# A hybrid convolution and attention block on one core: spectrum, values and output gates laid out in DRAM by the order of their loads

## The chip, the cores and the metric

The kernel runs on one core of a Trainium2 chip. The metric is the device time of one execution in microseconds (us), the median over several runs. The engines are TensorE (PE, matrix products), VectorE (DVE), ScalarE (ACT), GpSimd (POOL) and SyncE (SP). SP issues nearly all transfers between DRAM and the on-chip memory; ACT issues a few. Sixteen DMA engines carry them out, in packets of one contiguous run each.

## The reference

One block works on 2048 tokens of width 1024, with 256 context tokens and a conditioning vector. Half of the width goes through a gated long convolution, the other half through gated linear attention (4 heads, keys of 64, values of 128, both directions). Then come an output projection and an MLP of 4096.

```
spec = _hyena_spectrum(T, ...)        # rfft of a generated filter of 512 channels
u, q, k, v, og, gk = split(h @ w_in)  # widths 1536, 256, 256, 512, 512, 16+16
y1 = x0 * (irfft(rfft(x1 * v1) * spec) + bias)
y2 = gla_bidir(q, k, v, log_gate(gk)) normalized * silu(og)
x  = x + gate * ([y1, y2] @ w_out)
x  = x + gate * (relu(norm(x) @ w1)**2 @ w2)
```

## The kernel before, in words

Matrix products that need full precision are made of three products of rounded halves (`mm3`, lines 226 to 228). The stages, in time: the spectrum of the filter with the context beside it (0 to 232 us), the projections (226 to 821), the convolution with the attention woven in (821 to 1126), the output projection (to 1400), the MLP (to the end). Each stage is written as Python generators that take turns by weights; a scheduler then orders each engine's instructions within that, and pools of buffers with a fixed count set how far a load can run ahead.

**Spectrum.** `kernel_steps` goes twice over 256 of the 512 channels (`hc`). In 16 steps each it makes two blocks of 128 frequency rows, `ks` (line 640), 128 partitions by 2 x 256 numbers, and stores them to the DRAM tensor `d_s` (line 649). Rows 0 to 63 of a block are real parts, rows 64 to 127 imaginary parts. `d_s` is `[32, 128, 512]`: block, row, channel. The first step (`t == 0`) stores its blocks apart: row 127 of block 0 goes to `d_s0` and is filled with zeros in `d_s` (lines 644, 645), rows 0 to 126 of block 0 by line 646, and block 1 by line 647.

**Values, gates.** The columns of the input projection for values (512), output gates (512) and decay gates (32) are held as four groups of 264, `wi_vg`. `token_major` multiplies each group with 16 blocks of 128 tokens; a value goes to `d_v`, an output gate through Silu (ACT, line 694) and a product with the norm's weights (POOL, line 695) to `d_og`, both `[2048, 512]`, token by column. Since 264 does not divide 512, group 1 holds 248 columns of values and 16 of gates, and group 3 holds the 32 decay columns, copied to `gs` (line 698).

**Convolution.** For each half of the channels: a forward transform (`ua1`, `ua2`), a loop of 16 steps over the frequency blocks, an inverse transform. A step of the loop is staged over `k0` (loads), `k1`, `k2`, `k3`. `k0` loads the transforms' coefficients `dff` and `dfi` at every second step (lines 917, 919), and the step's spectrum to two tiles, `kr` and `ki`, of 128 partitions by 512 numbers (lines 923, 924). Both halves of a tile's partitions hold the same 64 rows, so there are four loads a step, each of 64 partitions by 2 runs of 256 numbers. `k2` makes the forward product on PE (`pu`, line 945), then `kr*pu` on DVE (line 951), `sw*ki` on POOL (line 952) and their sum on DVE (line 953); `k3` is the inverse product on PE (`p`, line 962). There are 5 buffers for `kr`, 3 for `ki`, 2 for `dff`, 3 for `dfi`.

**Attention.** In turns with that, for each of 4 heads: `kt` and `vv` (keys, values) are loaded once (1 MB each, lines 826 and 830), `qi`, `ki<-d_ki` and `dc` (lines 1055 to 1058), and for each quarter of the tokens the gates `og` (256 KB, line 1112). The loads of `vv` and `og` read 128 numbers of a token at a time.

All these loads stand in one queue on SP, in program order. A load that waits, for its buffer for one, holds all that stand behind it. Besides, each transfer takes one of eight semaphores in turn and waits until the transfer eight places ahead of it has landed.

Of the kernel before, what the change touches and what calls it, by code (L numbers as in the profile page):

```python
# [124 lines left out]
def layout(x):  # L125

    f4 = np.float32
    c = constants()
    x = {k: np.asarray(v) for k, v in x.items()}
    o = {"x": x["x"][0], "ctx": x["ctx"][0], "norm_final": x["norm_final"], "gla_norm": x["gla_norm"][0],  # L130
         "w_out": x["w_out"][0]}
    col = lambda v: v.reshape(-1, P).T
    prm = np.zeros((P, NPRM), f4)
    for at, v in ((SILC, x["c"]), (SILC + 8, x["c_ctx"]), (B_ADA, x["b_ada"]), (NMIX, x["norm_mix"]),
                  (NMLP, x["norm_mlp"]), (CONVW, x["conv_w"]), (CONVB, x["conv_b"]), (HB, x["hyena_bias"]),
                  (GKB, x["gk_b_fwd"]), (GKB + 2, x["gk_b_bwd"])):
        v = col(v)
        prm[:, at:at + v.shape[1]] = v
    for i, nm in enumerate(("filt_b1", "filt_b2", "filt_b3", "filt_freq")):
        prm[:64, FLT + i] = prm[64:, FLT + i] = x[nm][0]  # L140
    prm[:, TKC:TKC + 32] = c["tk"]
    prm[:, IDC:IDC + P] = c["ident"]
    o["prm"] = prm
    fpk = np.zeros((P, 1536), f4)
    for i, nm in enumerate(("filt_w1", "filt_w2", "filt_w3")):
        w = x[nm][0]
        n = w.shape[0]
        fpk[0:n, i * P:i * P + 64] = w
        fpk[n:2 * n, i * P + 64:(i + 1) * P] = w
    fpk[:64, 384:896] = x["filt_wout"][0][:, :DH]  # L150
    fpk[64:, 384:896] = x["filt_wout"][0][:, DH:]
    fpk[:, 896:1024] = c["dft_k"]
    fpk[:, 1024:1536] = c["negdelta"]
    o["fpk"] = fpk
    gw = np.zeros((P, 2, 256), f4)
    for i in range(4):
        gw[32 * i:32 * i + 16, 0] = x["gk_w_fwd"][0]
        gw[32 * i + 16:32 * i + 32, 1] = x["gk_w_bwd"][0]
    o["gw"] = gw
    blk = lambda w: np.ascontiguousarray(w.reshape(-1, P, w.shape[1]).transpose(1, 0, 2))  # L160
    wa = x["w_ada"][0]
    o["wada1"] = np.stack([blk(wa[:, i * 256:(i + 1) * 256]) for i in range(8)])
    o["wada2"] = np.stack([blk(wa[:, 2 * D + i * P:2 * D + (i + 1) * P]) for i in range(32)])
    wi = x["w_in"][0]
    o["wi_vg"] = np.stack([blk(wi[:, 2048 + i * 264:2048 + (i + 1) * 264]) for i in range(4)])
    two = lambda a, b: np.concatenate([blk(wi[:, a:a + P]), blk(wi[:, b:b + P])], axis=2)
    o["wi_qk"] = np.stack([two(1536 + i * P, 1792 + i * P) for i in range(2)])
    o["wi_xv"] = np.stack([two(512 + i * P, 1024 + i * P) for i in range(4)])
    o["wi_x0"] = np.stack([blk(wi[:, i * P:(i + 1) * P]) for i in range(4)])

    w1 = x["w_mlp1"][0].reshape(2, 4, P, 16, 2, P)
    o["w1"] = np.stack([np.stack([w1[l, :, :, n, i].transpose(1, 0, 2).reshape(P, 512)
                                  for i, l in ((0, 0), (0, 1), (1, 1), (1, 0))], axis=1) for n in range(16)])

    w2 = x["w_mlp2"][0].reshape(16, 2, P, 2, 512)
    o["w2"] = np.stack([np.stack([w2[n, i, :, j] for i, j in ((0, 0), (1, 0), (1, 1), (0, 1))], axis=1)
                        for n in range(16)])
    for n in ("zt", "dft_u", "dft_f", "dft_i", "dft_y", "reset", "attm"):
        o[n] = c[n]
    return {k: np.ascontiguousarray(v) for k, v in o.items()}  # L180
# [30 lines left out]
def hybrid_block(ctx: ExitStack, tc, a, out, dbg=None):  # L211
# [20 lines left out]
        dve.tensor_sub(lo, src, hi.bitcast(F32))  # L232

    dr = ctx.enter_context(tc.tile_pool(name="dram", bufs=1, space=DRAM))
    d_s = dr.tile([32, 128, DH], F32, name="d_s")
    d_s0 = dr.tile([1, DH], F32, name="d_s0")
    d_q = dr.tile([2, 256, T], F32, name="d_q")
    d_ki = dr.tile([2, 256, T], F32, name="d_ki")
    d_kt = dr.tile([NH, P, 16, 2, 64], F32, name="d_kt")
    d_dec = dr.tile([2, 256, 32], F32, name="d_dec")  # L240
    d_v = dr.tile([T, 512], F32, name="d_v")
    d_og = dr.tile([T, 512], F32, name="d_og")
    d_u = dr.tile([DH, T], F32, name="d_u")
    d_x0 = dr.tile([DH, T], F32, name="d_x0")
    d_yt = dr.tile([D, T], F32, name="d_yt")
# [108 lines left out]
    with ExitStack() as ek:  # L354
# [114 lines left out]
        def context_steps():  # L469
# [11 lines left out]
            yield from norm_out(xc, hch, hcl, 1)  # L481
            vc = xp.tile([P, 2, 512], F32, name="vc")
            gc = xp.tile([P, 2, 32], F32, name="gc")
            for g_, c0, n in ((3, 232, 32), (0, 0, 264), (1, 0, 264)):
                hi, lo = load_w(a["wi_vg"][g_][:, :, c0:c0 + n])
                for i in range(2):
                    pp = pt("pc")
                    for k in range(KD):
                        ts = slice(i * P, (i + 1) * P)
                        mm3(pp[:, 0:n], hch[:, k, ts], hcl[:, k, ts], hi[:, k, 0:n], lo[:, k, 0:n],  # L490
                            k == 0, k == KD - 1)
                    if g_ == 0:
                        nc.scalar.copy(vc[:, i, 0:264], pp[:, 0:264])
                    elif g_ == 1:
                        nc.scalar.copy(vc[:, i, 264:512], pp[:, 0:248])
                    else:
                        nc.scalar.copy(gc[:, i, :], pp[:, 0:32])
                    yield W["c_proj"]
# [57 lines left out]
        def kernel_steps():  # L556
            for hc in range(2):
# [73 lines left out]
                def second(t):  # L631
# [10 lines left out]
                    if t == 0:  # L642

                        dma(d_s0[:, cs], k3[127:128, 0, :])
                        dma(d_s[0, 127:128, cs], zrow[0:1, :])
                        dma(d_s[0, 0:127, cs], k3[0:127, 0, :])
                        dma(d_s[1, :, cs], k3[:, 1, :])
                    else:
                        dma(d_s[kk:kk + 2, :, cs].rearrange("k p c -> p k c"), k3)

                yield from staged(16, fetch, turn, second, w=W["k_turn"])

# [16 lines left out]
    rst = ap.tile([P, 512], F32, name="rst")  # L669
    dma(rst[:], a["reset"])  # L670

    def token_major(grp, w, tbs):

        c0 = 264 * grp
        hi, lo = w
        vn = max(0, min(264, 512 - c0))
        on = min(1024 - c0, 264) - vn
        o0 = max(0, c0 - 512)
        for tb in tbs:
            if grp == 3:  # L680
                gs = ap.tile([P, 4, 32], F32, tag="gs", bufs=2, name="gs")
            for i in range(4):
                pp = pt("pv")
                ts = slice(i * P, (i + 1) * P)
                for k in range(KD):
                    mm3(pp[:, 0:264], hts[tb][0][:, k, ts], hts[tb][1][:, k, ts], hi[:, k, :], lo[:, k, :],
                        k == 0, k == KD - 1)
                rows = slice(tb * 512 + i * P, tb * 512 + (i + 1) * P)
                st = ap.tile([P, 512], F32, tag=("gt1", "glg")[i % 2], bufs=2, name="st")
                if vn:  # L690
                    dve.tensor_copy(st[:, 0:vn], pp[:, 0:vn])
                    dma(d_v[rows, c0:c0 + vn], st[:, 0:vn])
                if on:
                    act(st[:, vn:vn + on], pp[:, vn:vn + on], AF.Silu)
                    gps.tensor_mul(st[:, vn:vn + on], st[:, vn:vn + on], gnf[:, o0:o0 + on])
                    dma(d_og[rows, o0:o0 + on], st[:, vn:vn + on])
                if grp == 3:
                    dve.tensor_copy(gs[:, i, :], pp[:, 232:264])
                yield 2.7
            if grp == 3:  # L700
                pg = pt("pg")
                for i in range(4):
                    tr(pg[0:32, i * P:(i + 1) * P], gs[:, i, :], ident)
                dve.tensor_copy(gt[tb * 32:(tb + 1) * 32, :], pg[0:32, :])

    def mod_block(j):
# [116 lines left out]
    def load_kv(h, part=None):  # L823
        if part != 1:
            kt = pre.tile([P, 16, 2, 64], F32, tag="kt", bufs=1, name="kt")
            dma(kt[:], d_kt[h])
            heads[h, "kt"] = kt
        if part != 0:
            vv = gpool(h).tile([P, 16, P], F32, tag="vv", bufs=1, name="vv")
            dma(vv[:], d_v[:, h * P:(h + 1) * P].rearrange("(b p) e -> p b e", p=P))  # L830
            heads[h, "kv"] = (heads[h, "kt"], vv)

    def load_u(ct):
# [48 lines left out]
    def conv_steps():  # L882
        for hc in range(2):
# [29 lines left out]
            def k0(t):  # L913
# [4 lines left out]
                    st["i", t // 2] = ft("dfi", 3, "dfi")  # L918
                    dma(st["i", t // 2][:], a["dft_i"][:, kk:kk + 4, :].rearrange("p k n -> p (k n)"))
                kr, ki = ft("kr", 5, "kr"), ft("ki", 3, "ki")  # L920
                for h in range(2):
                    hs = slice(h * 64, (h + 1) * 64)
                    dma(kr[hs].rearrange("p (k c) -> p k c", k=2), d_s[kk:kk + 2, 0:64, cs].rearrange("k p c -> p k c"))
                    dma(ki[hs].rearrange("p (k c) -> p k c", k=2), d_s[kk:kk + 2, 64:128, cs].rearrange("k p c -> p k c"))
                if t == 0:
                    dma(kr[127:128, 0:256], d_s0[:, cs])
                st["k", t] = (kr, ki)
# [181 lines left out]

    def load_og(h, q):  # L1110
        og = gp.tile([P, 4, P], F32, tag="og", bufs=4, name="og")
        dma(og[:], d_og[q * DH:(q + 1) * DH, h * P:(h + 1) * P].rearrange("(b p) e -> p b e", p=P))
        heads[h, "og", q] = og

    def outputs(h, q):
# [654 lines left out]
```

## Time and profile before

| | |
|---|---|
| median of 3 runs | 2690.08 us (2682.15 to 2690.41) |
| the profiled execution | 2681.11 us, of which its span 2679.3 us |
| granted PE clock, mean | 0.963 |
| PE busy | 2497.2 us (93%) |
| DVE, ACT, POOL busy | 1613.7, 1186.3, 1077.1 us |
| moved by DMA | 406.09 MB in 304480 packets |
| loads of `kr`, `ki` from `d_s` | 64 + 64 of 128 KB, median 4.1 and 5.4 us from issue to landing |

Instructions are named by line, engine, operation and tile: `L945 PE MATMUL pu<-zt,dff` writes `pu` from `zt` and `dff` at line 945. `SPq` is SP's queue of issues; the time of such an entry is that of issuing, and the time to landing is given apart. In the list of waits a line names who waited, for whom, the total in us, how often and the longest. In the view by stretches each engine has its busy time and its count of instructions, then follow the granted clock of PE, the busy share of the sixteen DMA engines and GB/s. "x4" joins four instructions in a row.

### The profile page before, as it was taken

To read this page: it belongs to the slowest core of one execution; us is meant where nothing else is said; L and a number is where in the kernel's file an instruction comes from. 1 tells how busy PE (TensorE), PEld (TensorE's weight loads), DVE (VectorE), ACT (ScalarE), POOL (GpSimd) and SP (SyncE) were. 2 spreads that over 40 slices of the span, in tenths; PEclk is the share of its full clock that TensorE was granted. 3 is DMA by queue.
4 is the path that set the end of the run, shared out by engine and by line. 5 is a ranking of instruction groups with operands and counts; after the bars stand their busy time and mean duration, and the time that the engine had idled before them with its cause. 6 is when DMAs were issued, how large, how long until landed. Compare 5 with 4: busy or idle time off the path is not lost. (4 is left out here: it accounts for less than half of the span.)

```text
span 2679.3 us, 38019 instructions
## 1 busy us (share of the span) xinstructions
PE 2497.2 (93%) x13320; PEld 2068.7 (77%) x13320; DVE 1613.7 (60%) x2619; ACT 1186.3 (44%) x2273; POOL 1077.1 (40%) x1093
## 2 busy tenths in 40 slices
PE   9799999999998788899989998999978999998997
PEld 5678978898887777788778887888857777777776
DVE  5754366735567677744465557555565656565668
ACT  6464352225225555434555555555543333333334
POOL 2130231214112223132244443544456666666575
PEclk9899999999998798899999999999989999999999
DMA  5425444432547777556444545545474233323233
GB/s 195 147 80 175 124 135 141 139 110 98 175 148 198 202 242 199 198 164 212 154 149 138 165 139 169 170 140 165 135 285 151 99 114 105 119 101 114 99 132 135
DMA packets 304480, 406.09 MB, mean 152 GB/s; under 512 B 25108, under 2 KB 226712, under 8 KB 293920
## 3 DMA queue, kind: packets, MB, share of 16 engines
q1 hardware_dynamic: 301408, 395.27, 46.7%
q10 hardware_dynamic: 2880, 8.39, 0.8%
q8 instruction: 105, 1.72, 0.3%
q14 instruction: 87, 0.71, 0.1%
HBM read 273.49 MB, written 130.09 MB: 151 GB/s over the span
## 5 line engine op out<-in xcount | busy, mean ns | idle before, releaser
L1598 POOL TENSOR_TENSOR ul<-ur,uh 128x256 fp32r<-128x256 f32 x441 | 362.5, 830 | 209.6 <-ACT uh L1597 208.3
L1645 DVE TENSOR_TENSOR acc<-acc,ps 128x512 f32<-128x512 f32 x448 | 303.8, 682 | 153.4 <-PE ps L1640 150.4
L1597 ACT CAST uh<-ur 128x256 fp32r<-128x256 f32 x448 | 179.8, 406 | 408.8 <-PE ps L1640 387.5
L1384 PE MATMUL ps<-bh,wh 128*128 128x512 f32 x896 | 350.4, 393 | 5.8 <-ACT u L1392 3.1
L1384 PE MATMUL ps<-bl,wh 128*128 128x512 f32 x896 | 351.0, 392 | 4.1 <-DVE bl L232 4.1
L1384 PE MATMUL ps<-bh,wl 128*128 128x512 f32 x896 | 350.4, 392 | 4.1 <-DVE wl L232 4.1
L232 DVE TENSOR_TENSOR wl<-raw,wh 128x512 fp32r<-128x512 f32 x276 | 266.7, 978 | 97.0 <-ACT wh L231 94.2
L231 ACT CAST wh<-raw 128x512 fp32r<-128x512 f32 x276 | 170.6, 622 | 201.8 <-PE ps L1384 165.5
L1640 PE MATMUL ps<-wh,uh 128*128 128x512 f32 x448 | 183.5, 410 | 66.4 <-DVE acc L1645 58.2
L1384 PEld LDWEIGHTS ps<-bh,wh 128*128 128x128 f32 x896 | 169.6, 189 | 43.0 <-ACT u L1392 3.7
L1384 PEld LDWEIGHTS ps<-bh,wl 128*128 128x128 f32 x896 | 169.3, 189 | 40.7 <-DVE wl L232 5.3
L1384 PEld LDWEIGHTS ps<-bl,wh 128*128 128x128 f32 x896 | 169.3, 189 | 40.2 <-DVE bl L232 5.3
L1640 PE MATMUL ps<-wh,ul 128*128 128x512 f32 x448 | 179.4, 400 | 0.3 <-DVE ul L1598 0.2
L1640 PE MATMUL ps<-bh,uh 128*128 128x512 f32 x448 | 179.5, 401 | 0.0
L1640 PE MATMUL ps<-bl,uh 128*128 128x512 f32 x448 | 179.5, 401 | 0.0
L1640 PE MATMUL ps<-wl,uh 128*128 128x512 f32 x448 | 179.2, 400 | 0.0
L1640 PE MATMUL ps<-bh,ul 128*128 128x512 f32 x448 | 179.0, 400 | 0.0
L1640 PEld LDWEIGHTS ps<-wh,uh 128*128 128x128 f32 x448 | 87.8, 196 | 96.0 <-DVE acc L1645 63.3
L226 PE MATMUL ph<-hth,whi 128*128 128x512 f32 x384 | 150.9, 393 | 0.0
L226 PE MATMUL pv<-whi,hth 128*128 128x264 f32 x512 | 147.2, 288 | 2.8 <-ACT whi L231 2.6
L228 PE MATMUL ph<-hth,wlo 128*128 128x512 f32 x384 | 149.6, 390 | 0.2 <-DVE wlo L232 0.2
L227 PE MATMUL ph<-htl,whi 128*128 128x512 f32 x384 | 149.4, 389 | 0.0
(289 smaller groups left out, 5713.1 us busy)
## 6 DMA issues: line engine op xcount, KB each, us to landing
raw<-in_w_dram SPq DMA_DIRECT2D x49, 1024.0 KB, 5.5
ur<-d_m SPq DMA_DIRECT2D x112, 448.0 KB, 3.7
d_m<-c SPq DMA_DIRECT2D x128, 256.0 KB, 2.5
d_m<-s SPq DMA_DIRECT2D x96, 256.0 KB, 3.4
xt<-in_x_dram SPq DMA_DIRECT2D x32, 512.0 KB, 5.0
mwt<-in_wada_dram SPq DMA_DIRECT2D x64, 256.0 KB, 3.0
raw<-in_wi_vg_dram SPq DMA_DIRECT2D x20, 528.0 KB, 4.8
wada<-in_wada_dram SPq DMA_DIRECT2D x16, 512.0 KB, 7.6
```

Source lines behind the costliest of these rows:

```text
L226: mm(ps, lh, rh, start=first, stop=False)
L227: mm(ps, lh, rl, start=False, stop=False)
L228: mm(ps, ll, rh, start=False, stop=last)
L231: nc.scalar.copy(hi, src)
L232: dve.tensor_sub(lo, src, hi.bitcast(F32))
L1384: mm(ps[:], x_[:, sl], y_[j], start=start and i == 0, stop=stop and i == 2, skip_group_check=True)
L1597: nc.scalar.copy(hi[:], src)
L1598: (gps if at else dve).tensor_sub(lo[:], src, hi[:].bitcast(F32))
L1640: mm(ps[:], x_[:, kb, :], y_[:], start=start and kb + i == 0, stop=kb == 1 and i == 2, skip_group_check=True)
L1645: dve.tensor_add(acc(t, i, j), acc(t, i, j), ps[:])
```

## The change

Three DRAM layouts and one grouping of columns change. What is computed stays.

- `d_s` becomes `[2, 16, 128, 2, 256]`: half of the channels, step, row, block, channel. A step's store writes 2 KB a partition in one run. `kr` and `ki` are loaded by one DMA each, whose source names the 64 rows twice.
- `d_v` and `d_og` become `[4, 128, 16, 128]`: head, token within its block, block, column. A partition of `vv` reads 8 KB in one run, one of `og` 2 KB. The stores write 128 numbers at a time to two heads.
- A group of `wi_vg` holds 256 value or output gate columns and 8 of the decay gates. `gs` becomes one tile, filled by a copy of 8 columns in each of 64 token blocks. For the context, 256 of the 264 columns of groups 0 and 1 are loaded, and the 32 decay columns from an array of their own, `wi_gk`.

```
-    d_s = dr.tile([32, 128, DH], F32, name="d_s")
+    d_s = dr.tile([2, 16, 128, 2, 256], F32, name="d_s")
-    d_v = dr.tile([T, 512], F32, name="d_v")
-    d_og = dr.tile([T, 512], F32, name="d_og")
+    d_v = dr.tile([NH, P, 16, P], F32, name="d_v")
+    d_og = dr.tile([NH, P, 16, P], F32, name="d_og")
...
-    o["wi_vg"] = np.stack([blk(wi[:, 2048 + i * 264:2048 + (i + 1) * 264]) for i in range(4)])
+    o["wi_vg"] = np.stack([two(2048 + i * 256, 3072 + i * 8, 256, 8) for i in range(4)])
+    o["wi_gk"] = blk(wi[:, 3072:3104])
...
-                        dma(d_s[kk:kk + 2, :, cs].rearrange("k p c -> p k c"), k3)
+                        dma(d_s[hc, t], k3)
...
-                if vn:
-                    dve.tensor_copy(st[:, 0:vn], pp[:, 0:vn])
-                    dma(d_v[rows, c0:c0 + vn], st[:, 0:vn])
-                if on:
-                    act(st[:, vn:vn + on], pp[:, vn:vn + on], AF.Silu)
-                    gps.tensor_mul(st[:, vn:vn + on], st[:, vn:vn + on], gnf[:, o0:o0 + on])
-                    dma(d_og[rows, o0:o0 + on], st[:, vn:vn + on])
-                if grp == 3:
-                    dve.tensor_copy(gs[:, i, :], pp[:, 232:264])
+                if grp < 2:
+                    dve.tensor_copy(st[:, 0:256], pp[:, 0:256])
+                else:
+                    act(st[:, 0:256], pp[:, 0:256], AF.Silu)
+                    gps.tensor_mul(st[:, 0:256], st[:, 0:256], gnf[:, (grp - 2) * 256:(grp - 1) * 256])
+                hs = slice(2 * (grp % 2), 2 * (grp % 2) + 2)
+                dma((d_v, d_og)[grp // 2][hs, :, 4 * tb + i, :].rearrange("h p e -> p h e"),
+                    st[:, 0:256].rearrange("p (h e) -> p h e", h=2))
+                dve.tensor_copy(gs[:, tb, i, 8 * grp:8 * grp + 8], pp[:, 256:264])
...
-            dma(vv[:], d_v[:, h * P:(h + 1) * P].rearrange("(b p) e -> p b e", p=P))
+            dma(vv[:], d_v[h])
...
-                for h in range(2):
-                    hs = slice(h * 64, (h + 1) * 64)
-                    dma(kr[hs].rearrange("p (k c) -> p k c", k=2), d_s[kk:kk + 2, 0:64, cs].rearrange("k p c -> p k c"))
-                    dma(ki[hs].rearrange("p (k c) -> p k c", k=2), d_s[kk:kk + 2, 64:128, cs].rearrange("k p c -> p k c"))
+                for v, hs in ((kr, slice(0, 64)), (ki, slice(64, 128))):
+                    dma(v[:], d_s[hc, t, hs].rearrange("p k c -> p (k c)").partition_broadcast(2))
...
-        dma(og[:], d_og[q * DH:(q + 1) * DH, h * P:(h + 1) * P].rearrange("(b p) e -> p b e", p=P))
+        dma(og[:], d_og[h, :, 4 * q:4 * q + 4, :])
```

PE's order stays, except for the width of the context's products. On SP the start of the first spectrum loop reads so before (each row is a line, the tile written and its source, partitions by numbers; `x2` is two in a row):

```order
L917 DMA dff<-in_dft_f_dram 128x512
L919 DMA dfi<-in_dft_i_dram 128x512
L923 DMA kr<-d_s 64x2x256
L924 DMA ki<-d_s 64x2x256
L923 DMA kr<-d_s 64x2x256
L924 DMA ki<-d_s 64x2x256
L923 DMA kr<-d_s 64x2x256
L924 DMA ki<-d_s 64x2x256
L926 DMA kr<-d_s_58 1x256
L923 DMA kr<-d_s 64x2x256
L924 DMA ki<-d_s 64x2x256
L917 DMA dff<-in_dft_f_dram 128x512
```

And the same place after the change:

```order
L912 DMA dff<-in_dft_f_dram 128x512
L914 DMA dfi<-in_dft_i_dram 128x512
L917 DMA kr<-d_s 128x1x512
L917 DMA ki<-d_s 128x1x512
L917 DMA kr<-d_s 128x1x512
L917 DMA ki<-d_s 128x1x512
L919 DMA kr<-d_s_58 1x256
L912 DMA dff<-in_dft_f_dram 128x512
```

Two steps of four half loads have become two steps of two whole loads; the second `dff` stands six places behind the first load instead of ten. The other place is the change from the first half of the channels to the second, on SP too. Before:

```order
L835 DMA uc<-d_u 128x2048
L1112 DMA og<-d_og 128x4x128
L917 DMA dff<-in_dft_f_dram 128x512
L919 DMA dfi<-in_dft_i_dram 128x512
L923 DMA kr<-d_s 64x2x256
L924 DMA ki<-d_s 64x2x256
L923 DMA kr<-d_s 64x2x256
L830 DMA vv<-d_v 128x16x128
L1056 DMA qi<-d_q 64x2048 x2
```

After:

```order
L830 DMA uc<-d_u 128x2048
L912 DMA dff<-in_dft_f_dram 128x512
L914 DMA dfi<-in_dft_i_dram 128x512
L917 DMA kr<-d_s 128x1x512
L917 DMA ki<-d_s 128x1x512
L917 DMA kr<-d_s 128x1x512
L917 DMA ki<-d_s 128x1x512
L919 DMA kr<-d_s_58 1x256
```

The gate load `og` and the values `vv` that stood between the input of the second half, `uc`, and its spectrum now come later, behind the first steps' spectrum.

More of the change, by code (lines that the diff above doesn't have):

```diff
@@ L164, in layout @@
     wi = x["w_in"][0]
-    o["wi_vg"] = np.stack([blk(wi[:, 2048 + i * 264:2048 + (i + 1) * 264]) for i in range(4)])
-    two = lambda a, b: np.concatenate([blk(wi[:, a:a + P]), blk(wi[:, b:b + P])], axis=2)
+    two = lambda a, b, n=P, m=P: np.concatenate([blk(wi[:, a:a + n]), blk(wi[:, b:b + m])], axis=2)
+    o["wi_vg"] = np.stack([two(2048 + i * 256, 3072 + i * 8, 256, 8) for i in range(4)])
+    o["wi_gk"] = blk(wi[:, 3072:3104])
     o["wi_qk"] = np.stack([two(1536 + i * P, 1792 + i * P) for i in range(2)])
@@ L483, in context_steps @@
             gc = xp.tile([P, 2, 32], F32, name="gc")
-            for g_, c0, n in ((3, 232, 32), (0, 0, 264), (1, 0, 264)):
-                hi, lo = load_w(a["wi_vg"][g_][:, :, c0:c0 + n])
+            for g_, n in ((2, 32), (0, 256), (1, 256)):
+                hi, lo = load_w(a["wi_gk"] if g_ == 2 else a["wi_vg"][g_][:, :, 0:n])
                 for i in range(2):
@@ L491, in context_steps @@
                             k == 0, k == KD - 1)
[L492 to L495, printed above, removed]
+                    if g_ < 2:
+                        nc.scalar.copy(vc[:, i, g_ * 256:(g_ + 1) * 256], pp[:, 0:256])
                     else:
@@ L644, in second @@
                         dma(d_s0[:, cs], k3[127:128, 0, :])
-                        dma(d_s[0, 127:128, cs], zrow[0:1, :])
-                        dma(d_s[0, 0:127, cs], k3[0:127, 0, :])
-                        dma(d_s[1, :, cs], k3[:, 1, :])
+                        dma(d_s[hc, 0, 127:128, 0], zrow[0:1, :])
+                        dma(d_s[hc, 0, 0:127, 0], k3[0:127, 0, :])
+                        dma(d_s[hc, 0, :, 1], k3[:, 1, :])
                     else:
-                        dma(d_s[kk:kk + 2, :, cs].rearrange("k p c -> p k c"), k3)
+                        dma(d_s[hc, t], k3)
                 yield from staged(16, fetch, turn, second, w=W["k_turn"])
@@ L670, in hybrid_block @@
     dma(rst[:], a["reset"])
+    gs = ap.tile([P, 4, 4, 32], F32, name="gs")
     def token_major(grp, w, tbs):
-        c0 = 264 * grp
         hi, lo = w
-        vn = max(0, min(264, 512 - c0))
-        on = min(1024 - c0, 264) - vn
-        o0 = max(0, c0 - 512)
         for tb in tbs:
-            if grp == 3:
-                gs = ap.tile([P, 4, 32], F32, tag="gs", bufs=2, name="gs")
             for i in range(4):
@@ L687, in token_major @@
                         k == 0, k == KD - 1)
-                rows = slice(tb * 512 + i * P, tb * 512 + (i + 1) * P)
                 st = ap.tile([P, 512], F32, tag=("gt1", "glg")[i % 2], bufs=2, name="st")
-                if vn:
-                    dve.tensor_copy(st[:, 0:vn], pp[:, 0:vn])
-                    dma(d_v[rows, c0:c0 + vn], st[:, 0:vn])
-                if on:
-                    act(st[:, vn:vn + on], pp[:, vn:vn + on], AF.Silu)
-                    gps.tensor_mul(st[:, vn:vn + on], st[:, vn:vn + on], gnf[:, o0:o0 + on])
-                    dma(d_og[rows, o0:o0 + on], st[:, vn:vn + on])
-                if grp == 3:
-                    dve.tensor_copy(gs[:, i, :], pp[:, 232:264])
+                if grp < 2:
[7 more added lines that the diff above has]
+                dve.tensor_copy(gs[:, tb, i, 8 * grp:8 * grp + 8], pp[:, 256:264])
                 yield 2.7
@@ L702, in token_major @@
                 for i in range(4):
-                    tr(pg[0:32, i * P:(i + 1) * P], gs[:, i, :], ident)
+                    tr(pg[0:32, i * P:(i + 1) * P], gs[:, tb, i, :], ident)
                 dve.tensor_copy(gt[tb * 32:(tb + 1) * 32, :], pg[0:32, :])
```

## The prediction

> **What bounds the kernel now.** I read the page first, then the stage in which the changed loads run.
>
> ```profile
> span 2679.3 us, 38019 instructions
> PE 2497.2 (93%) x13320; PEld 2068.7 (77%) x13320; DVE 1613.7 (60%) x2619; ACT 1186.3 (44%) x2273; POOL 1077.1 (40%) x1093
> ```
>
> TensorE (PE) is busy for 93% of the span, so 182 us are idle and a gain must come out of these. The view by stretches says how much of it lies where the change acts:
>
> ```profile
> core 0: us, PE busy (x) PEld busy (x) DVE busy (x) ACT busy (x) POOL busy (x), PEclk, DMA share, GB/s
> 821.00:843.00 22.00, 19.78 (x145) 16.36 (x143) 17.95 (x47) 16.36 (x30) 0.00 (x0) 1.00 0.85 203
> 843.00:920.00 77.00, 56.70 (x502) 49.47 (x503) 55.50 (x111) 42.52 (x80) 25.31 (x22) 0.80 0.88 235
> 920.00:991.00 71.00, 63.90 (x637) 57.05 (x637) 50.58 (x116) 32.39 (x58) 8.25 (x12) 0.93 0.77 241
> 991.00:1058.00 67.00, 55.01 (x537) 48.78 (x536) 48.79 (x95) 38.14 (x73) 29.16 (x28) 0.90 0.63 186
> 1058.00:1126.00 68.00, 60.86 (x622) 51.20 (x621) 52.86 (x114) 31.89 (x54) 10.28 (x14) 0.88 0.56 169
> ```
>
> The five rows are the FFT convolution with the attention woven in: its start, the spectrum loop of the first 256 channels, the inverse transform and the start of the next half, the second spectrum loop, the rest. PE waits 20 us in the first loop and 12 us in the second, and the sixteen DMA engines are busy for 0.88 of the first, the highest share of the five. What was waited for there:
>
> ```profile
> POOL sw L952 <- DMA ki<-d_s: 22.1, 5, 8.0
> PE pu L945 <- DMA dff<-in_dft_f_dram: 16.0, 3, 7.5
> PE p L962 <- DVE kr L953: 7.0, 2, 5.7
> PE pd L1074 <- DMA vv<-d_v: 2.8, 1, 2.8
> ```
>
> (Microseconds in all, times, the longest.) PE's waits are for a transfer, `dff`, or for the product that needs the spectrum `ki`. The loads behind that:
>
> ```profile
> L923 SPq DMA_DIRECT2D kr<-d_s x64: 573/597/1416, 824.6 to 1047.6; - x64
> L924 SPq DMA_DIRECT2D ki<-d_s x64: 573/597/5359, 825.6 to 1048.2; - x64
> ...
> L646 SPq DMA_DIRECT2D d_s<-ks x2: 240/242/244, 94.4 to 192.5; - x2
> L647 SPq DMA_DIRECT2D d_s<-ks x2: 1377/1891/2405, 94.7 to 192.8; - x2
> ```
>
> (Issue time in ns, least, median, most.) 128 half loads cost SyncE (SP) 0.6 us each, 2.4 us for the four of a step; the last two rows are stores of the spectrum's first step, for later. So today each loop is held a little by SP's queue and the transfers in it, and never for long.
>
> **The two whole loads of a step.** The edit merges four loads of 64 partitions (128 packets of 1 KB) into two of 128 partitions (128 packets of 2 KB). To fill 128 partitions from the 64 rows that are stored, the source is read as two copies: its outermost count is 2, then 64 rows, then 512 numbers. What decides the time of the change is how many of the sixteen engines such a load gets. The half loads have 64 rows outermost on both sides, `dff` 128. One store of the kernel before has an odd count: L646 above writes 127 rows of 1 KB, and this is what the transfers look like while it drains alone:
>
> ```profile
> GB/s 41 0 41 41 0 41 0 41 41 0 41 0 41 0 0 41 0 41 0 41 41 0 41 0 41 41 0 41 0 41 0 41 41 0 41 0 41 41 0 41
> DMA packets 26, 0.02 MB, mean 24 GB/s; under 512 B 3, under 2 KB 26, under 8 KB 26
> ...
> q1 hardware_dynamic: 26, 0.02, 7.1%
> ```
>
> This is the DMA view of 96.5 to 97.5 us, in slices of 25 ns. One packet begins every 43 ns or so (23 of 1 KB in 1 us), and 7.1% of sixteen engines is 1.1 engines: the store goes through a single engine. So the hardware does not spread 127 rows as 8, 8 and so on; it divides the outer count evenly, and 127 has no divisor to divide by. A lone load or store of 128 rows does use all:
>
> ```profile
> GB/s 229 229 360 426 426 262 426 459 393 295 393 263 33 0 0 0 0 0 0 0 0 0 0 0 0 0 0 0 0 0 0 0 0 0 0 0 0 0 0 0
> DMA packets 144, 0.26 MB, mean 105 GB/s; under 512 B 16, under 2 KB 16, under 8 KB 144
> ...
> q1 hardware_dynamic: 144, 0.26, 28.1%
> ```
>
> That is 342.0 to 344.5 us: 128 packets of 2 KB in 0.8 us at some 400 GB/s, and 28.1% of 16 x 2.5 us is 11.2 us for them, 87 ns a packet. The single engine's 43.5 ns for 1 KB is the same rate, 23.5 GB/s.
>
> With an outer count of 2 the same even division gives two engines. Each carries 64 packets, 64 x 87 ns = 5.57 us for a load, against 8 packets or 0.70 us if the load were spread. The Trainium skill says the same as a rule, on its page "DMA: Bandwidth & Descriptors", in the section on why a DMA increments its semaphore by 16: the number of engines is the largest up to 16 that divides the slowest count above 1 of both access patterns. By it the 127 rows take one engine, which the rows above show, and two copies ahead of 64 rows take two, which no row of this trace shows.
>
> Now the loops. The two engines also carry their sixteenth of all else:
>
> ```profile
> DMA packets 48271, 63.66 MB, mean 209 GB/s; under 512 B 4339, under 2 KB 38727, under 8 KB 45616
> ...
> kr<-d_s SPq DMA_DIRECT2D x64, 128.0 KB, 4.1
> ki<-d_s SPq DMA_DIRECT2D x64, 128.0 KB, 5.4
> ...
> dff<-in_dft_f_dram SPq DMA_DIRECT2D x16, 256.0 KB, 3.0
> ```
>
> (821 to 1126 us.) Without the 16.8 MB of the spectrum 46.9 MB are left, 2.93 MB an engine, 125 us at 23.5 GB/s. The 64 loads are 356 us. Together 481 us must pass through each of two engines in a stage that lasts 305 us: **+176 us** at the least, if these two never rest.
>
> They do rest, so I go by stretches. First loop: the loads begin at 824.6; 32 of them are 178 us; the rest moved in 821 to 920 us is 203 GB/s x 22 us + 235 x 77 = 22.6 MB, less 8.4 of spectrum, 14.2 MB, 38 us an engine. The last load lands near 1041 us, its products and matmuls end some 5 us later, where they now end at 920: **+125**. Then the 71 us of inverse transform, which PE fills by 63.90, stay as they are; the two engines have 17.1 MB less 2.1 of spectrum to share in, 40 us, so there is room for about 5 loads of the second half ahead of its loop (the buffers would take 6). Second loop: 27 loads are 150 us, the rest of its stretch (186 GB/s x 67 us less 6.3 MB) 16 us, the end 5: 171 where it is 67 now, **+104**. Sum **+229 us**. PE's own work in a loop, 57 us even at a clock of 0.80, lies well under 170 us and stays hidden, also at half the clock. The tail after 1058 us is unchanged.
>
> What waits in these loops: `dff` and the attention's loads are queued on SP among the slow loads, and a sixteenth of their packets stands in line in each of the two engines, so they land late too; that share is the 38 and 16 us of the sum. The waits for `dff` (16.0) and for `vv` (2.8) that PE has now disappear inside the longer loop and give nothing back.
>
> **The other edits.** `d_v` and `d_og` by head: the loads become runs of 8 and 2 KB instead of 512 B, the stores runs of 512 B instead of 1 KB; `d_s` is stored in 2 KB runs. Regrouping drops 16 sixteen-column pieces (activation, product, store) and turns 16 gate copies into 64 narrower ones.
>
> ```profile
> 94.00:232.00 138.00, 119.37 (x809) 99.86 (x808) 73.73 (x136) 79.05 (x163) 30.60 (x33) 0.94 0.50 154
> 226.00:821.00 595.00, 589.00 (x3374) 512.20 (x3373) 330.11 (x627) 194.31 (x327) 134.67 (x150) 0.99 0.42 134
> ...
> L698 DVE COPY gs<-pv x16: 183/192/193, 307.9 to 623.1; 128x32 f32<-128x32 f32 x16
> ...
> L694 ACT ACTIVATE st<-pv x48: 163/364/393, 245.0 to 622.7; 128x16 f32<-128x16 f32 x16, 128x264 f32<-128x264 f32 x16, 128x232 f32<-128x232 f32 x16
> ...
> ACT ks L640 <- DMA d_s<-ks: 17.0, 7, 4.4
> ```
>
> In the projections (226 to 821 us) PE is busy 589 of 595 us. 48 more copies at no more than 0.19 us are 9 us on VectorE (DVE), which rests for 265 us there; 16 activations of 0.16 us are 2.6 us less on ScalarE (ACT). Both lie beside PE: 0, from -2 to +2. The spectrum's stores hold ACT's `ks` for 17.0 us in the stage 94 to 232, but its loop ends beside other matmuls: 0, from -2 to +1. The context's matmuls lose 8 of 264 columns, under 1 us.
>
> **The rivals.** *The loads spread over sixteen engines* (the destination's 128 partitions decide, or the pattern is cut anew). Then SP has 64 issues of 0.6 us fewer, 38 us over both loops, the engines in the first loop are no longer full, and PE's waits for `dff`, `vv` and `kr` go in part. They come to 25.8 us, and after each the four matmuls run at half speed (2.05 us, against 1.03 in the run of steps without a wait):
>
> ```profile
> 860.49 2.05 PE L945 MATMUL pu<-zt,dff 128*128 128x256 f32 x4 [6.64 <-DMA dff<-in_dft_f_dram]
> ...
> 866.85 1.03 PE L945 MATMUL pu<-zt,dff 128*128 128x256 f32 x4
> ...
> 896.03 2.04 PE L945 MATMUL pu<-zt,dff 128*128 128x256 f32 x4 [7.50 <-DMA dff<-in_dft_f_dram]
> ```
>
> About half is kept, since DVE is busy 226 of the stage's 305 us and becomes what PE waits for: -15 us, from -28 to 0, about 2675 in the median. It decides if a load still lands in the 4 to 5 us of now. For it speaks that the destination is one plain block of 128 partitions; against it the 127 rows, which nothing cut anew. A rule of the Trainium skill stands behind this rival: the same page, under "Rules for kernel authors", advises one transfer of 128 partitions in place of two to halves; no run here compares them. *The same spread, and nothing is won*: the buffers and DVE hold the loops at their present length, 2690.
>
> *Two engines under load.* In 821 to 1126 us a packet took longer than in the quiet window:
>
> ```profile
> q1 hardware_dynamic: 45531, 55.17, 65.0%
> ```
>
> 65.0% of 16 x 305 us is 3172 us for 55.17 MB, 57 ns a KB or 115 ns for 2 KB. If the two engines carry their 64 packets at that, a load is 7.3 us and the 64 loads cost 112 us more: +341 us, about 3030. Against it: the other fourteen engines are then nearly idle, and the single engine kept its 43 ns.
>
> *SP as the limit*: the issue behind the store of 127 rows (L647) held SP for 1.4 and 2.4 us, ten times the 0.24 of that store itself, as if SP had to wait for room in the one engine's list. Two such issues a step are under 5 us, less than the 11 us of the engines, and a wait for room ends when the engine has drained: no time of its own.
>
> **How the numbers follow.** Two engines at the quiet price 0.73, under load 0.15, spread with a gain 0.09, spread with none 0.03. The sum is made on the profiled execution, 2681 us: 2910. The median of the three runs is 9 us above it, so I forecast 2915 us. The lower end is the gapless sum, 2857, less 12 us since part of the other traffic is in 8 KB packets that need less time: 2845. The upper end takes in most of the loaded price: 3020. This leaves out the 12 in 100 of the spread cases and some of the loaded one. About 8 us, 0.3%, is what a measurement of this kernel can tell from no change. Faster 0.09, same 0.03, slower 0.88.
>
> **What would show it.** In the profile after: `kr<-d_s` and `ki<-d_s` landing in over 20 us from issue with several queued, the loops at 160 to 200 us each with a DMA share far below 0.88 and some 60 to 110 GB/s, PE's clock lower there, POOL's `sw` or DVE's `kr` waiting for the two loads for most of each loop, the rest of the span within a few us of before. If they land in 5 us and the loops last 60 to 75 us, the even division of the outer count is wrong for a broadcast. If the loops last over 230 us each, the packet's price was too low.

## The result, and the profile after

The changed kernel takes 2940.57 us in the median (2935.81 to 2944.16, 4 runs), the kernel before 2687.86 us beside it: a ratio of 1.095, with a 95% interval from 1.093 to 1.097. The forecast was 2915 us, from 2845 to 3020. The profiled execution's span went from 2679.3 to 2933.9 us, by 254.6.

The top of the page after:

```profile
span 2933.9 us, 37849 instructions
## 1 busy us (share of the span) xinstructions
PE 2528.0 (86%) x13320; PEld 2094.2 (71%) x13320; DVE 1617.9 (55%) x2667; ACT 1184.4 (40%) x2257; POOL 1075.0 (37%) x1077
```

PE has the same 13320 instructions and 31 us more of busy time, at a mean granted clock of 0.926 in place of 0.963; its idle time went from 182 to 406 us. The view by stretches of the kernel after (cut at the first product of the first loop, the start of the inverse transform, the first product of the second loop and the end of that loop; the table of before is cut within 4 us of these events):

```profile
844.50:1048.10 203.60, 66.39 (x508) 57.72 (x509) 54.91 (x116) 43.25 (x82) 25.15 (x22) 0.64 0.34 103
1048.10:1151.40 103.30, 73.35 (x633) 64.06 (x633) 50.12 (x114) 32.40 (x59) 8.25 (x12) 0.78 0.49 154
1151.40:1317.00 165.60, 71.16 (x552) 62.20 (x552) 50.76 (x98) 39.28 (x75) 28.89 (x28) 0.69 0.29 88
1317.00:1382.00 65.00, 57.93 (x600) 48.41 (x599) 51.92 (x109) 31.17 (x50) 10.29 (x14) 0.89 0.44 144
```

From event to event, the first loop went from 79 us (842.9 to 922.3) to 204 with about as many PE instructions, its DMA share from 0.88 to 0.34, its GB/s from 235 to 103: far fewer bytes a second, and engines that mostly rest. The second loop shows the same. The stretch between them, where no spectrum is used, grew too, from 70 to 103 us.

The waits in 821 to 1382 us of the kernel after (who, for whom, us in all, times, the longest):

```profile
POOL sw L945 <- DMA ki<-d_s: 272.6, 26, 28.5
...
PE pu L938 <- DMA dff<-in_dft_f_dram: 188.6, 12, 34.4
...
DVE kr L944 <- DMA kr<-d_s: 62.5, 22, 7.2
```

POOL waited 22.1 us for `ki` before, now 272.6; PE 16.0 us for `dff`, now 188.6. `dff` is a load of 128 rows, as before, but it stands behind the spectrum, and not on SP alone. Before, it landed 3.0 us after the start of its issue. Here SP had issued one by 1008.3, and PE waited for it until 1018.3, 10 us longer (first SP's row, start and length of the issue, then PE's, with the wait in brackets):

```profile
1003.13 5.14 SPq L912 DMA_DIRECT2D dff<-in_dft_f_dram  x1
...
1018.26 2.04 PE L938 MATMUL pu<-zt,dff 128*128 128x256 f32 x4 [13.45 <-DMA dff<-in_dft_f_dram]
```

That fits what the prediction says of `dff`, that a part of its packets stands in line in the two engines: 10 us are about two loads of the spectrum at the price found below. The issues of the two whole loads (least, median, most ns):

```profile
L917 SPq DMA_DIRECT2D kr<-d_s x32: 493/941/7302, 826.2 to 1280.1; - x32
L917 SPq DMA_DIRECT2D ki<-d_s x32: 513/5196/8040, 826.9 to 1286.1; - x32
```

Before, an issue took 0.6 us. Now it often takes over 5 us, as if SP were held until there is room again. How SP goes through a stretch of the second loop (start, length in us):

```profile
1197.92 5.44 SPq L917 DMA_DIRECT2D ki<-d_s  x1
1203.46 5.15 SPq L917 DMA_DIRECT2D kr<-d_s  x1
1208.71 5.17 SPq L917 DMA_DIRECT2D ki<-d_s  x1
1213.98 5.35 SPq L825 DMA_DIRECT2D vv<-d_v  x1
```

One load each 5.3 us, and `vv`, which is no spectrum, is held like the rest. The DMA view of the kernel after for 1205 to 1230 us, in slices of 0.625 us:

```profile
DMA  1111111112111111111112913899999994111111
GB/s 52 46 52 46 49 49 46 49 49 79 46 49 49 49 49 49 49 49 49 49 49 105 361 49 102 259 347 341 341 324 265 272 243 125 52 52 46 52 52 56
```

Where only the spectrum moves, it is 49 GB/s, a seventh of the 347 that the row shows where `vv` comes over all sixteen. One engine alone had 24 GB/s in the prediction's row of the 127-row store; 49 is two of these. A load's 262144 bytes are 5.35 us at 49 GB/s, the period of SP's issues.

Beside other transfers a load takes longer. The ends of the waits for the last `kr` and `ki` of the first loop, while the other engines fetch `x`, `og` and `kt`, lie 7.5 us apart; the last two loads of the second loop, with `qi`, `ki<-d_ki` and `og` beside them, took 15.9 us together and not 10.7:

```profile
1035.88 0.69 DVE L944 TENSOR_TENSOR kr<-kr,pu 128x512 f32<-128x512 f32 x1 [2.06 <-DMA kr<-d_s]
...
1043.34 1.26 POOL L945 TENSOR_TENSOR sw<-sw,ki 128x512 f32<-128x512 f32 x1 [12.42 <-DMA ki<-d_s]
...
1295.10 1.26 POOL L945 TENSOR_TENSOR sw<-sw,ki 128x512 f32<-128x512 f32 x1 [8.65 <-DMA ki<-d_s]
1311.02 1.26 POOL L945 TENSOR_TENSOR sw<-sw,ki 128x512 f32<-128x512 f32 x1 [14.66 <-DMA ki<-d_s]
```

### The profile page after: what moved, and what is told of

Its sections match the earlier page's. It is cut to its first block, busy times and chain, and to the rows that moved or that the text cites. A ratio compares the mean times of both kernels' runs of the same rounds, so it can differ in the third digit from the quotient of the medians.

```text
span 2933.9 us, 37849 instructions
## 1 busy us (share of the span) xinstructions
PE 2528.0 (86%) x13320; PEld 2094.2 (71%) x13320; DVE 1617.9 (55%) x2667; ACT 1184.4 (40%) x2257; POOL 1075.0 (37%) x1077
## 5 line engine op out<-in xcount | busy, mean ns | idle before, releaser
L1591 POOL TENSOR_TENSOR ul<-ur,uh 128x256 fp32r<-128x256 f32 x441 | 365.2, 836 | 203.9 <-ACT uh L1590 203.6
L234 DVE TENSOR_TENSOR wl<-raw,wh 128x512 fp32r<-128x512 f32 x276 | 269.2, 987 | 96.6 <-ACT wh L233 94.0
L938 PE MATMUL pu<-zt,dff 128*128 128x256 f32 x128 | 48.3, 515 | 189.2 <-DMA dff<-in_dft_f_dram 188.6
L938 PEld LDWEIGHTS pu<-zt,dff 128*128 128x128 f32 x128 | 30.0, 260 | 196.2 <-issue 191.3
L945 POOL TENSOR_TENSOR sw<-sw,ki 128x512 f32<-128x512 f32 x32 | 40.8, 1274 | 349.5 <-DMA ki<-d_s 272.6
```

Source lines behind the costliest of these rows:

```text
L938: mm(pu[:, s * 256:(s + 1) * 256], dff[:, q * P:(q + 1) * P], zt[:, s * 256:(s + 1) * 256], start=True, stop=True)
L945: gps.tensor_mul(sw[:], sw[:], ki[:])
L1591: (gps if at else dve).tensor_sub(lo[:], src, hi[:].bitcast(F32))
```

## The experiments

Ratios are to the kernel before on the same chip. The first theory: a pattern gets as many engines as divide its outermost count, and the two copies ahead of the 64 rows leave two. Its rivals: the repeated reading itself is slow; loads of this kind are slow whatever their count; the other layouts have a part in the loss.

**The spectrum's part alone**, on the kernel before:

```
-    d_s = dr.tile([32, 128, DH], F32, name="d_s")
+    d_s = dr.tile([2, 16, 128, 2, 256], F32, name="d_s")
-                        dma(d_s[kk:kk + 2, :, cs].rearrange("k p c -> p k c"), k3)
+                        dma(d_s[hc, t], k3)
...
+                    dma(v[:], d_s[hc, t, hs].rearrange("p k c -> p (k c)").partition_broadcast(2))
```

> The kernel before with the spectrum's layout and its two loads of two copies a step, and nothing else of the change. Theory (two engines for a source whose outermost count is 2): the whole loss is here, 2930 to 2960 us. Rival (part of the loss comes from the other layouts or the regrouped columns): under 2850 us.

2937.5 us, ratio 1.092 (1.083 to 1.102). The whole loss is in this part.

**62 and 2 rows, 60 and 4 rows, 57 and 7 rows.** On the changed kernel, no repeated source; each half tile is cut in two:

```
-                for v, hs in ((kr, slice(0, 64)), (ki, slice(64, 128))):
-                    dma(v[:], d_s[hc, t, hs].rearrange("p k c -> p (k c)").partition_broadcast(2))
+                for h in range(2):
+                    for v, r in ((kr, 0), (ki, 64)):
+                        for b, e in ((0, 62), (62, 64)):      # 60 and 57 in the others
+                            dma(v[h * 64 + b:h * 64 + e, :], d_s[hc, t, r + b:r + e].rearrange("p k c -> p (k c)"))
```

> The changed kernel without any repeated source: each half tile is loaded as 62 rows and 2 rows, eight loads a step. Theory (the outer count decides, 62 has no divisor up to 16 above 2): 62 rows go through two engines, a step again puts 128 packets of 2 KB on each of them, the time stays near the changed kernel's, 2900 to 2980 us, and the DMA share in the loops stays low. Rival (reading the same rows twice in one transfer is what is slow): fast, 2670 to 2730 us.

> The same with 60 rows and 4 rows, as many loads and bytes. Theory: 60 rows go through 15 engines, 4 through 4, so the loss is gone: 2670 to 2730 us (eight issues a step may cost something against the kernel before). Rival (many or small loads, or two loads of the same rows, are what is slow): as slow as with 62 and 2, within 30 us of it.

> As with 62 and 2 rows, now 57 rows and 7 rows. Theory (largest count up to 16 that divides): 57 rows go through three engines, 19 packets each, the 7 rows through seven, one each. A step puts 80 packets on each of three engines instead of 128 on two, 7.0 us instead of 11.1. The first loop then lasts 111 + 38 us after its loads begin, some 135 to 150 us (204 in the changed kernel), the second 95 to 115, the whole 2770 to 2830 us. Rival (a count that doesn't divide by 16 falls to one or two engines, whatever it is): as slow as 62 and 2 or slower, 2900 us and more.

| rows of a load | us | ratio | first loop, us |
|---|---|---|---|
| two copies of 64 (the change) | 2940.57 | 1.095 | 203.6 |
| 62 and 2 | 2917.61 | 1.085 (1.075 to 1.095) | 204.4 |
| 57 and 7 | 2786.84 | 1.038 (1.034 to 1.042) | 141.8 |
| 60 and 4 | 2710.11 | 1.010 (1.007 to 1.012) | 96.7 |
| 64 (before) | 2687.86 | 1 | 79.4 |

The loops of the three cut kernels, as rows of their views by stretches; first 62 and 2:

```profile
845.00:1049.40 204.40, 66.02 (x509) 56.96 (x509) 59.39 (x136) 43.44 (x82) 25.33 (x22) 0.63 0.34 104
```

57 and 7:

```profile
844.20:986.00 141.80, 66.96 (x508) 57.68 (x508) 62.95 (x136) 43.38 (x82) 25.33 (x22) 0.68 0.47 146
```

60 and 4:

```profile
844.50:941.20 96.70, 57.47 (x509) 48.81 (x509) 66.07 (x136) 43.17 (x82) 25.57 (x22) 0.85 0.70 210
```

All three issue as many loads and move the same bytes. Two rows more in a load than 60 make the loop twice as long, three fewer make it half as long again. What moves while only the spectrum is loaded shows why. GB/s in the second loop, slices of 0.375 us, with 62 and 2 rows (1195 to 1210 us):

```profile
GB/s 49 49 49 49 49 49 49 49 49 76 366 317 44 55 44 55 44 55 49 49 49 55 49 49 49 49 49 49 49 49 49 49 49 49 49 44 87 180 213 300
```

and with 57 and 7 (1110 to 1125 us):

```profile
GB/s 76 76 71 76 87 82 175 322 290 268 273 137 87 82 82 66 82 66 98 71 76 71 98 71 76 71 76 93 76 66 71 98 71 76 71 131 82 76 71 77
```

49 GB/s is the changed kernel's rate without any repeated source; 71 to 76 is three engines of 24.5. 62 has 2 as its largest divisor up to 16, 57 has 3, 60 has 15. The rule that the prediction took from the Trainium skill, page "DMA: Bandwidth & Descriptors", in the section on why a DMA increments its semaphore by 16, is borne out by all of these. The traces also record every update of a transfer's semaphore: there are 3 for a load of two copies or of 62 rows, 4 for 57 rows, 5 for 4 rows, 8 for 7 rows, and 16 for 60 or 128 rows, one more than the rule's number of engines wherever that is under 16. That a repeated reading is slow in itself is out; so is a fall to one or two engines for every odd count. The 17 us that 60 and 4 rows lose in the first loop against four loads of 64 may be the 15 engines or the eight transfers a step, which take turns at the same eight semaphores; this isn't told apart. SP's own time is not it: eight issues at a median of 0.31 us are 2.5 us a step, four at 0.6 us were 2.4.

**Why the stretch between the loops grew.** ACT's rows in the kernel after gave a first theory for the 33.6 us that the forecast didn't have. These stand behind three of its stores to `d_yt`:

```profile
1081.23 0.60 ACT L1131 ACTIVATE oq<-po 128x512 f32<-128x512 f32 x1 [13.58 <-DMA dfi<-in_dft_i_dram]
...
1094.41 1.07 ACT L980 COPY zy<-py 128x512 f32<-128x512 f32 x2 [8.61 <-DMA ki<-d_s]
...
1113.67 0.60 ACT L1131 ACTIVATE oq<-po 128x512 f32<-128x512 f32 x1 [9.59 <-DMA kr<-d_s]
```

A store from ACT waits until the transfer eight places ahead has landed; that is now a slow load of the next half's spectrum, or a `dfi` behind one, and the copies behind the store, which PE needs, are held 31.8 us in all. Three runs followed this, each with one thing more taken off ACT or SP:

```
-    put_out = nc.scalar.dma_start
+    put_out = nc.gpsimd.dma_start                               # stores_by_pool
...
-            dma(vv[:], d_v[h])
+            nc.gpsimd.dma_start(vv[:], d_v[h])                  # vv_by_pool, besides
...
-        dma(uc[:], d_u[ct * P:(ct + 1) * P, :])
+        nc.gpsimd.dma_start(uc[:], d_u[ct * P:(ct + 1) * P, :]) # inputs_by_pool, besides
...
-                dma(x0[:], d_x0[ct * P:(ct + 1) * P, :])
+                nc.gpsimd.dma_start(x0[:], d_x0[ct * P:(ct + 1) * P, :])
```

> The changed kernel with the stores of the convolution's and the attention's results issued by GpSimd in place of ScalarE. Theory on the stretch between the two spectrum loops, which went from 70 to 103 us: ScalarE's stores stand behind a transfer eight places earlier, a slow spectrum load, and hold the copies behind them; without them on its queue the stretch is 70 to 80 us and the kernel 2905 to 2920 us. Rival (the stretch is long since its own loads come late): the stretch stays at 95 to 105 us, 2935 to 2945 us in all. GpSimd's own products could be held instead; then the loops grow.

2935.5 us, ratio 1.091 (1.080 to 1.103). ACT's waits were gone, and the stretch still lasted 102.3 us. PE now waited in one piece:

```profile
1119.59 2.08 PE L1067 MATMUL pd<-vv,kt 64*128 64x128 f32 x16 [29.32 <-DMA vv<-d_v]
```

So the theory of ACT's stores fell: they were one of several things held, and without them the next was as late. `vv` was issued on SP behind the eight spectrum loads that the buffers let run ahead, and after its issue it was waited for another 20 us:

```profile
1095.76 3.69 SPq L825 DMA_DIRECT2D vv<-d_v  x1
```

> The changed kernel with the results' stores and the values' loads issued by GpSimd. Theory (between the loops PE waits 29 us for vv since its load stands on SP behind the second half's slow spectrum loads): the wait for vv falls under 10 us and the stretch of 102 us by 15 us or more. The second loop may give part of it back, since its loads are that much less ahead: 2905 to 2930 us in all. Rival (the two engines' backlog holds vv, whoever issues it): the wait stays above 20 us, 2930 to 2945 us.

2942.26 us, ratio 1.096 (1.091 to 1.100), the stretch 103.2 us: a miss for the total and the stretch, not for the wait. Issued by POOL, `vv` landed in 8 to 11 us and PE did not wait for it; it waited for the next load on SP:

```profile
1134.38 1.09 PE L890 MATMUL pa<-prm,uc 128*128 128x128 f32 x4 [35.34 <-DMA uc<-d_u]
```

> As the last, with the convolution's inputs (uc and x) issued by GpSimd too; the spectrum, the transforms and the attention's other loads stay on SP. In the run before this one the wait for vv was gone and PE waited 35 us for uc, issued on SP at 69 us after the stretch began (45 in the kernel before). Theory (the stretch is long since SP's one queue brings what PE needs next behind the second half's spectrum): uc is issued 20 us earlier, the stretch falls from 103 to 70 to 90 us, the second loop stays at 160 to 175 us, 2910 to 2930 us in all. Rival (the two engines are the bound over stretch and loop together): what the stretch gains the second loop loses, 2935 to 2945 us.

2920.75 us, ratio 1.089 (1.083 to 1.096). The stretch runs from the start of the first of these rows to that of the last:

```profile
1055.84 1.88 PE L978 MATMUL py<-prm,za 128*128 128x128 f32 x8 [0.61 <-DVE za L959]
1091.95 1.99 PE L902 MATMUL pb<-ua,ut 128*128 128x256 f32 x8 [0.28 <-ACT ut L892]
1108.20 1.09 PE L890 MATMUL pa<-prm,uc 128*128 128x128 f32 x4 [6.89 <-DMA uc<-d_u]
...
1127.43 1.13 PE L938 MATMUL pu<-zt,dff 128*128 128x256 f32 x4 [0.40 <-ACT zt L930]
```

71.6 us, against 69.7 in the kernel before, with the spectrum as slow as ever. The loops give some of it back: the first lasts 210 us in place of 204, the second 4 us more. So the stretch was long because SP's one queue brought what PE needed next behind the slow loads, both at the issue and after it.

**What the edits are worth without the two copies.**

```
-                for v, hs in ((kr, slice(0, 64)), (ki, slice(64, 128))):
-                    dma(v[:], d_s[hc, t, hs].rearrange("p k c -> p (k c)").partition_broadcast(2))
+                for h in range(2):                              # half_loads, on the changed kernel
+                    for v, r in ((kr, 0), (ki, 64)):
+                        dma(v[h * 64:h * 64 + 64, :], d_s[hc, t, r:r + 64].rearrange("p k c -> p (k c)"))
```

> The changed kernel with four half loads a step from the new layout, 64 rows of 2 KB each, 64 outermost on both sides. Theory (only the outer count of 2 was slow): the loss is gone and what the prediction's gain rival held is left of the other edits, 2665 to 2690 us, the loops 60 to 80 us each. Rival (the regrouping or the stores cost too): 2690 to 2720 us.

> The changed kernel with the spectrum's layout and its four half loads of 1 KB runs as before: only values, gates and the regrouped columns. Theory: these are worth little, 2675 to 2692 us, and PE's wait for vv is under 3 us. Rival (the regrouping costs copies on VectorE): 2692 to 2710 us.

> The kernel before with the spectrum's layout alone and four half loads of 2 KB runs. Theory: the loops' DMA share falls and PE waits less for dff: 2670 to 2690 us. Rival (SP's issues, not the packets, hold the loops, and their number is unchanged): within 5 us of before.

The last two have one part of that kernel each: the first the old `d_s` and its loads, the second only the new `d_s` with the half loads above.

| | us (11 runs each) | ratio |
|---|---|---|
| half loads from the new layout, all else as changed | 2680.60 | 0.9973 (0.9954 to 0.9991) |
| values, gates, columns alone | 2679.96 | 0.9978 (0.9960 to 0.9995) |
| spectrum's layout alone, half loads | 2683.79 | 0.9994 (0.9976 to 1.0011) |

Half loads in place of the two copies beat both kernels, by 7 us against before. The values and gates bring as much alone; the spectrum's 2 KB runs alone can't be told from nothing. That time lies in the ranges of both its theory and its rival, so the run does not decide between them. In the profile of the half loads PE's longest sum of waits in 821 to 1126 us is still this one, which was 16.0:

```profile
PE pu L939 <- DMA dff<-in_dft_f_dram: 13.4, 3, 6.4
```

**Whole loads of 128 stored rows.** The spectrum is stored twice, so that 128 rows lie in one block:

```
-    d_s = dr.tile([2, 16, 128, 2, 256], F32, name="d_s")
+    d_s = dr.tile([2, 16, 2, 2, 64, 512], F32, name="d_s")
...
-                        dma(d_s[hc, t], k3)
+                        for h in range(2):
+                            for r in range(2):
+                                dma(d_s[hc, t, r, h], ks[64 * r:64 * r + 64, :])
...
-                    dma(v[:], d_s[hc, t, hs].rearrange("p k c -> p (k c)").partition_broadcast(2))
+                    dma(v[:], d_s[hc, t, r].rearrange("h p c -> (h p) c"))
```

> The changed kernel with the spectrum's rows stored twice, so that a step's two loads of 128 partitions read 128 rows each, 256 KB in one block, no copies in the pattern. Four stores of 64 rows a step in place of one, 8 MB more written. Theory: two loads of 128 rows go over sixteen engines and save 64 issues, so this is at or below the half loads, 2655 to 2685 us, if the stores lie beside PE's work. Rival (the number of loads doesn't matter any more, and the spectrum stage pays for the stores): 3 to 20 us above the half loads.

2699.39 us, ratio 1.005 (1.003 to 1.007): the theory missed, and the rival's cost in the spectrum stage came. From the first product of the loops to the last inverse product it took 202.4 us (873.4 to 1075.8), 13.4 less than before (842.9 to 1058.7). PE's wait for `dff` there fell to 3.7 us. But the stage that stores the spectrum lost more:

```profile
L637 PE MATMUL pu<-zt,dff x128: 379/379/765, 92.8 to 250.8; 128*128 128x256 f32 x128
```

Its last products started at 226.5 us before, at 250.8 now: +24. The stores take 0.6 us each on SP, eight of them for two steps, ahead of the next `dff`:

```profile
98.63 2.38 SPq L653 DMA_DIRECT2D d_s<-ks  x4
101.12 0.54 SPq L618 DMA_DIRECT2D dff<-in_dft_f_dram  x1
103.21 4.95 SPq L653 DMA_DIRECT2D d_s<-ks  x8
108.67 0.34 SPq L618 DMA_DIRECT2D dff<-in_dft_f_dram  x1
```

To tell SP's time from the doubled bytes, the second copy's stores went to POOL:

```
-                                dma(d_s[hc, t, r, h], ks[64 * r:64 * r + 64, :])
+                                (nc.gpsimd.dma_start if h else dma)(d_s[hc, t, r, h], ks[64 * r:64 * r + 64, :])
```

> The spectrum stored twice, the second copy's two stores of a step issued by GpSimd instead of SP; whole loads of 128 rows. Theory: with SP alone eight stores of 0.6 us for two steps stood ahead of the transforms' dff and cost 24 us in the spectrum stage; half of them gone, at least 15 of these come back, the convolution stays 13 us shorter than before: 2672 to 2688 us. Rival (the doubled bytes hold the stage, not SP): the stage keeps its 24 us, 2695 to 2705 us.

2696.08 us, ratio 1.004 (1.003 to 1.006), a miss. The stage's last products still started at 246.5 us; only 4 of the 24 came back, PE still waited 18.5 us for `dff` there (28.2 with one queue, 8.3 before), and POOL waited 56.6 us in order for `ks` to be ready for its stores. My theory of SP's eight issues explains a small part at most. Whether the bytes or the order of the stores hold the stage stays open.

## Why the prediction was right

Where the 254.6 us lie, from the profiles, against the terms of the sum:

| | before | after | more | predicted |
|---|---|---|---|---|
| first loop | 79.4 | 203.6 | 124.2 | 125 |
| stretch between | 69.7 | 103.3 | 33.6 | 0 |
| second loop, to its last inverse product | 66.8 | 163.4 | 96.6 | 104 |
| all else | | | 0.2 | 0 |

- **Two engines for two copies**: right. It was reasoned from a store of 127 rows; 49 GB/s, and the same rate with 62 rows, show it.
- **The price of a load**: 5.57 us forecast, 5.35 measured where only the spectrum moves. "Two engines under load", at 7.3 us, came for the few loads beside which much else moved (7.5 us at the end of the first loop, 15.9 for the two at the end of the second), and not for most of them.
- **The first loop**: right within 1 us, in part by luck. From the first load's issue at 826.2 to the end of the wait for the last at 1043.3 it is 217 us. Of these 32 loads at 5.35 are 171, 7 less than forecast; all else took 46, where the sum had 38.
- **The second loop**: 7 us less than forecast, and again two errors partly cancel. Eight loads ran ahead where I had five, and room for six; the 24 left are 128 us, not 150. But SP issued the first of them 4.7 us into the loop, at 1156.1, and from there to the end of the wait for the last, at 1311.0, it is 155 us: all else took 27 us and not 16.
- **The signs named**: DMA shares of 0.34 and 0.29 in the loops, 103 and 88 GB/s, clocks of 0.64 and 0.69, and 23 us from the issue of the first loop's last `ki` (1020.4) to the end of the wait for it came as named. The first loop's 204 us is just over its 160 to 200.
- **The step that failed**: "the 71 us of inverse transform, which PE fills by 63.90, stay as they are". I counted what the two engines could carry in that time and not who stands behind those loads. In the rival on SP I even wrote that a wait for room is "no time of its own". In the loops that holds, since the engines are the bound there. In the stretch between, SP is what PE depends on for `vv`, `uc` and, over the eight semaphores, ACT's stores; it was held 5 us a load, and what it had issued landed late too. That is the 33.6 us, shown by taking the loads off SP. The total missed the sum by 26 us only, since the two loops were 8 us shorter than forecast.
- **The other edits**: 0, from -2 to +2 each, was right for the changed kernel outside the convolution ("all else" is 0.2 us). Without the two copies they bring 7 us, from 1 to 11 by the interval of the values and gates alone.
- **The rival that loads spread**: it was wrong for this change, and its -15 us for the convolution was a fair price: whole loads of 128 stored rows gave -13.4 there.

## What to carry to other kernels

Before two transfers are made into one, look at what then stands outermost on each side: the engines that it gets follow from that count, and a repeated source of two copies gets two. When a queue is to carry slow loads, price not only the loads but everything that stands behind them on that queue, in stretches that use none of their data too. A repeated block can keep its 64 rows outermost in two loads, at 0.6 us of issue each.

## What the runs showed that I had not expected

A load confined to two engines can hold the issuing queue itself: SP's issue went from 0.6 us to a median of 5.2 us for `ki`, so a slow transfer delays loads that don't wait for it by any semaphore. Two engines alone are not enough for that. With 62 and 2 rows, at the same 49 GB/s, SP's issues were short (least, median, most ns, below), and the stretch between the loops, with `vv` and `uc` on SP as before, lasted 75.9 us and not 103.3:

```profile
L919 SPq DMA_DIRECT2D kr<-d_s x128: 222/257/2162, 826.7 to 1274.7; - x128
L919 SPq DMA_DIRECT2D ki<-d_s x128: 222/242/2293, 829.1 to 1278.0; - x128
```

Eight transfers, as many as the semaphores let stand in line, put 128 packets on each of the two engines there, and 512 with the whole loads. That SP was held for this reason is my estimate; no run tests it.

The outer count's divisors act finely: 57 rows run at 71 to 76 GB/s, 62 rows at 49. And with the stores by POOL the wait moved without getting smaller, 31.8 us on ACT, then 29.3 us for `vv`, then 35.3 us for `uc`, until all three stood on POOL.
